# Relieving one DMA engine of 48 scattered rows, and marking the engines with fifteen small loads

## The chip, the cores and the metric

The kernel runs on one core of one Trainium2 chip. The metric is the device time of an execution in microseconds (us). Times are medians of several executions; a profile is one execution and gives the span from its first to its last instruction, some 2 us less than the timed value. Every timed run used below is in the fast state; a single look, which has too few runs to be placed, is marked so.

The engines are PE (matmul), DVE (vector), ACT, POOL (GpSimd) and SP (sync). The profile counts sixteen DMA engines. The trace records every DMA packet with its queue, its size and its duration, but not the number of its engine. A row that is copied from HBM to HBM (10,240 bytes) shows up as 16 packets of 640 bytes and 16 of 4 bytes (768 rows on q10 are 12,288 of each in the kernel before), which I read as one of each on every engine, the small one for its semaphore. A row that is scattered is one packet of 10,240 bytes (116 scatters of 128 rows are 14,848), and so on one engine.

## The reference

```python
x = np.random.randn(8, 2048, 2560).astype(np.float32)
scores = np.random.randn(8, 2048).astype(np.float32)
order = np.argsort(scores, axis=1)
ranks = np.argsort(order, axis=1)
out[b_idx, ranks, :] = x          # each row goes to the place of its rank
```

Every row of x (10,240 bytes) is read once and written once, to a place that is known only when the rank is known. That is 168 MB read and 168 MB written, so the kernel lives on its DMA engines.

## The kernel before

Each batch of 2048 rows is cut into eight groups of 256. Group 0 of batches 0 to 5 goes HBM to HBM, row by row, issued by SP and ACT (768 rows each, queues q1 and q10). The other 58 groups ("tiles") go through SBUF: POOL loads 128 partitions of 2 rows each, then scatters them in two indirect DMAs of 128 rows (queue q0). The ranks are counted by DVE.

```python
    GROUPS = [(256 * i, 2) for i in range(8)]
    DIRECT = range(6)
    BULK = [(b, g) for b in range(B) for g in range(len(GROUPS)) if g or b not in DIRECT]
    NBUF = 8
    LAG = 4
    G = 16
    ...
        for b in DIRECT:
            for h, (line, name) in enumerate(((sp, ENG.SP), (act, ENG.Activation))):
                line.after(dve, t_rows[b])
                half = WIDE // 2
                with line.eng.Fori(0, half // G) as q:
                    _, at = nc.values_load_multi_w_load_instructions(rows_i[b][...], ...)
                    for i in range(G):
                        row = b * N + GROUPS[0][0] + half * h + i
                        line.eng.dma_start(
                            out=out_bytes[bass.ds(at[i], ROW)],
                            in_=x_bytes[bass.ds(q * (G * ROW) + row * ROW, ROW)],
                        ).then_inc(s_rows[line], 16)
        for line in (sp, act):
            line.wait(s_rows[line], 16 * len(DIRECT) * WIDE // 2)
    ...
        def scatter(k, j):
            ...
            nc.gpsimd.indirect_dma_start(
                out=out_flat,
                out_offset=bass.IndirectOffsetOnAxis(ap=rank_i[:, col:col + 1], axis=0),
                in_=xb[k % NBUF][:, j * D:(j + 1) * D],
                in_offset=None,
                element_offset=b * N * D,
            ).then_inc(s_scat[k % NBUF][j], 16)
    ...
        for k, (b, g) in enumerate(BULK):
            i = k % NBUF
            if k >= LAG and k + NBUF - LAG < len(BULK):
                scatters_done(pl, k - LAG)
                load(pl, k + NBUF - LAG, s_load[(k - LAG) % NBUF])
            ...
            for j in range(GROUPS[g][1]):
                scatter(k, j)
        nc.gpsimd.drain()

        for k in range(max(0, len(BULK) - NBUF), len(BULK)):
            scatters_done(sp, k)
```

Of the kernel before, what the change touches and what calls it, by code (L numbers as in the profile page):

```python
# [7 lines left out]
P = 128  # L8
F32 = mybir.dt.float32
BF16 = mybir.dt.bfloat16  # L10
I32 = mybir.dt.int32
U8 = mybir.dt.uint8
OP = mybir.AluOpType
ENG = mybir.EngineType
# [26 lines left out]
def kernel(  # L41
# [6 lines left out]
    nc = tc.nc  # L48
    B, N, D = x.shape
    C = N // P  # L50
    ROW = 4 * D
# [4 lines left out]
    GROUPS = [(256 * i, 2) for i in range(8)]  # L56
    DIRECT = range(6)
    MMAX = max(m for _, m in GROUPS)
    WIDE = GROUPS[0][1] * P
    BULK = [(b, g) for b in range(B) for g in range(len(GROUPS)) if g or b not in DIRECT]  # L60
    NBUF = 8
    LAG = 4
    G = 16

    STEPS = [(0, 1), (1, 2), (2, 4), (4, 8)]

    def first_col(g):
        return GROUPS[g][0] // P if g < len(GROUPS) else C
# [11 lines left out]
    acc = [pool.tile([P, B * C], F32, name=f"acc{i}") for i in range(3)]  # L80
    rank = pool.tile([P, B * C], F32, name="rank")
    rank_i = pool.tile([P, B * C], I32, name="rank_i")
    rows_i = {b: pool.tile([1, WIDE], I32, name=f"rows_i{b}") for b in DIRECT}
    xb = [pool.tile([P, MMAX * D], F32, name=f"x{i}") for i in range(NBUF)]
    ps_col = psum.tile([P, 512], F32, name="ps_col")
# [7 lines left out]
    with tc.tile_critical(no_gpsimd_drain=True):  # L93
# [9 lines left out]
            [nc.alloc_semaphore(f"scat{i}_{j}") for j in range(MMAX)]  # L103
            for i in range(NBUF)
        ]
        s_rows = {sp: nc.alloc_semaphore("rows_sp"), act: nc.alloc_semaphore("rows_act")}
        n_scat = [[0] * MMAX for _ in range(NBUF)]

# [66 lines left out]
        def broadcast(b):  # L175
            pe.after(dve, t_copied)
            ticks = []
            for c in range(C):
                pe.did(
                    nc.tensor.transpose(  # L180
                        out=ps_all[:, P * c:P * (c + 1)],
                        in_=s_col[:, c, b:b + 1].to_broadcast([P, P]),
                        identity=ident[:],
                    )
                )
                if c % 4 == 3:
                    ticks.append(pe.n)
            return ticks
# [3 lines left out]
        dve.after(pl, t_mask)  # L192
        bc = broadcast(0)

        def ranks(b, g_lo, g_hi):

            for g in range(g_lo, g_hi):
                lo = first_col(g)
                m = GROUPS[g][1]
                for j in range(m):  # L200
                    col = b * C + lo + j
                    score = s_col[:, lo + j, b:b + 1]
                    dve.after(dve, dve.n)

                    def count(i, lo_c, hi_c, do, **how):
                        dve.did(
                            do(  # L207
                                out=trash[i][:, :P * (hi_c - lo_c)],
                                in0=s_all[:, P * lo_c:P * hi_c],
                                accum_out=acc[i][:, col:col + 1],  # L210
                                **how,
                            )
                        )

                    count(
                        0, lo, C, nc.vector.tensor_scalar,
                        scalar1=score, scalar2=None, op0=OP.is_lt, op1=OP.add,
                    )
                    if lo:
                        count(  # L220
                            1, 0, lo, nc.vector.tensor_scalar,
                            scalar1=score, scalar2=None, op0=OP.is_le, op1=OP.add,
                        )
                    count(
                        2, lo, lo + m, nc.vector.scalar_tensor_tensor,
                        scalar=score,
                        in1=mask[:, MMAX - j:MMAX - j + m, :].rearrange("p a b -> p (a b)"),
                        op0=OP.is_equal, op1=OP.mult,
                    )
            cols = slice(b * C + first_col(g_lo), b * C + first_col(g_hi))  # L230
            dve.after(dve, dve.n)
            dve.did(
                nc.vector.tensor_tensor(  # L233
                    out=rank[:, cols], in0=acc[0][:, cols], in1=acc[1][:, cols], op=OP.add
                )
            )
            dve.after(dve, dve.n)
            dve.did(
                nc.vector.tensor_tensor(  # L239
                    out=rank[:, cols], in0=rank[:, cols], in1=acc[2][:, cols], op=OP.add  # L240
                )
            )
            dve.after(dve, dve.n)
            tick = dve.did(
                nc.vector.tensor_copy(out=rank_i[:, cols], in_=rank[:, cols])  # L245
            )
            for g in range(g_lo, g_hi):
                t_bulk[b, g] = tick

        def rows_to_psum(b):  # L250
            pe.after(dve, dve.n)
            for j in range(GROUPS[0][1]):
                pe.did(
                    nc.tensor.transpose(  # L254
                        out=ps_row[:1, P * j:P * (j + 1)],
                        in_=rank[:, b * C + j:b * C + j + 1],
                        identity=ident[:],
                    )
                )

        def rows_to_bytes(b):
            dve.after(pe, pe.n)
# [11 lines left out]
        for b in range(B):  # L274
            dve.after(dve, dve.n)
            for q in range(4):
                dve.after(pe, bc[q])
                t_copied = dve.did(
                    nc.vector.tensor_copy(  # L279
                        out=s_all[:, 512 * q:512 * (q + 1)],  # L280
                        in_=ps_all[:, 512 * q:512 * (q + 1)],
                    )
                )
            steps = STEPS if b == 0 else [(0, len(GROUPS))]
            for lo, hi in steps:
                ranks(b, lo, hi)
                if lo == 0:
                    if b in DIRECT:
                        rows_to_psum(b)
                        rows_to_bytes(b)  # L290
                    if b + 1 < B:
                        bc = broadcast(b + 1)


        for b in DIRECT:
# [4 lines that stand above are left out]
                    _, at = nc.values_load_multi_w_load_instructions(  # L300
                        rows_i[b][:, bass.ds(half * h + q * G, G)],
                        engines=[name],
                        min_val=b * N * ROW,
                        max_val=(b * N + N - 1) * ROW,
                        skip_runtime_bounds_check_because=(
                            "a rank counts other scores of one batch of N, so it lies in 0..N-1"
# [5 lines that stand above are left out]
                            out=out_bytes[bass.ds(at[i], ROW)],  # L312
                            in_=x_bytes[bass.ds(q * (G * ROW) + row * ROW, ROW)],
                        ).then_inc(s_rows[line], 16)
        for line in (sp, act):
            line.wait(s_rows[line], 16 * len(DIRECT) * WIDE // 2)


        def scatters_done(line, k):
# [4 lines left out]
        def scatter(k, j):  # L324
            b, g = BULK[k]
            col = b * C + first_col(g) + j
            n_scat[k % NBUF][j] += 1
# [3 lines that stand above are left out]
                in_=xb[k % NBUF][:, j * D:(j + 1) * D],  # L331
                in_offset=None,
                element_offset=b * N * D,
            ).then_inc(s_scat[k % NBUF][j], 16)

        for k in range(1, NBUF):
            load(pl, k, s_load[k])
        for k, (b, g) in enumerate(BULK):
            i = k % NBUF
            if k >= LAG and k + NBUF - LAG < len(BULK):  # L340
                scatters_done(pl, k - LAG)
                load(pl, k + NBUF - LAG, s_load[(k - LAG) % NBUF])
            if k == 0:
                pl.wait(s_first, 16)
            else:
                pl.wait(s_load[i], 16 * (k // NBUF + (i > 0)))
            pl.after(dve, t_bulk[b, g])
            for j in range(GROUPS[g][1]):
                scatter(k, j)
        nc.gpsimd.drain()  # L350

        for k in range(max(0, len(BULK) - NBUF), len(BULK)):
            scatters_done(sp, k)

# [29 lines left out]
```

## Time and profile before

| | before |
|---|---|
| median of 2 runs | 793.37 us (792.85 to 793.88) |
| profiled span | 791.4 us |
| last scatter packet ends | 786.68 us |
| landings of a scatter near 757 us, against the middle one: first, 15th, 16th | -0.9, +3.4, +23.1 us |
| packets of 10,240 bytes (scatters) | 14,848, mean 386.8 ns |
| one row: 640-byte packet, its 4-byte packet | 32 ns, 9 ns |

The third row and those below it are read from the packet records and the semaphore landings, not from the page. A scatter's semaphore has 16 landings, read here as one by each of the 16 engines, so they show how far apart the engines are. (A scatter is named here by the time of its middle landing; how far the last one is behind that is called its lag.) Here fourteen are together, one is 3 to 4 us behind, one is 23 us behind. The page's slices and the stretches that belong to this are shown inside the prediction. Two further lines are needed later. The first is from the waits of SP (line, releaser: total us, times, longest): at the end SP waits 2.9 us in the closing barrier for POOL.

```profile
SPq L93 <- POOLq L93: 2.9, 1, 2.9
```

The second is a stretch in the middle. Its columns are the stretch, its length, the busy time of PE, PEld, DVE, ACT and POOL, the granted clock, the DMA share, and GB/s.

```profile
395.00:406.00 11.00, 0.00 (x0) 0.00 (x0) 10.86 (x25) 0.00 (x0) 2.70 (x3) 0.50 1.01 419
```

The DMA engines are full there: share 1.01, 419 GB/s. (The share is the packets' time over that of 16 engines; a packet starts some 3 ns before the one ahead of it ends, so full engines read a little over 1.) That is the ordinary rate of this kernel.

### The profile page before, as it was taken

How to read it: one execution, taken by the hardware profiler on the slowest of the kernel's cores; microseconds unless marked ns; L12 is line 12 of the kernel's file. 1: busy time of each engine (PE TensorE's matmuls, PEld its weight loads, DVE VectorE, ACT ScalarE, POOL GpSimd, SP SyncE). 2: the span in 40 equal slices, each digit the busy share in tenths (PEclk: the TensorE clock that was granted, in tenths of full speed). 3: DMA queues.
4: the chain of work that ended last, by engine and by line, in shares of the span. 5: the costliest groups of instructions: out<-in, count | busy, mean ns of one | idle time of the engine just before them, and what ended most of it. 6: DMA issues, size and time to landing. Idle time of an engine off the chain costs nothing.

```text
span 791.4 us, 7991 instructions
## 1 busy us (share of the span) xinstructions
PE 30.9 (4%) x156; PEld 27.6 (3%) x156; DVE 398.3 (50%) x809; ACT 0.0 (0%) x1; POOL 146.2 (18%) x182
## 2 busy tenths in 40 slices
PE   4000010020100200200000000000000000000000
PEld 3000010010100100200000000000000000000000
DVE  5999999999999999999992000000000000000000
ACT  0000000000000000000000000000000000000000
POOL 2114021212121211112121212121111212121000
PEclk9655555555555555655555555555555555555555
DMA  8999999999999999999999999999999999999960
GB/s 366 423 407 416 425 416 423 418 425 415 427 414 425 415 424 416 425 420 422 419 419 421 420 422 420 422 418 423 418 424 419 422 419 423 418 425 418 417 252 19
DMA packets 74239, 320.12 MB, mean 404 GB/s; under 512 B 27368, under 2 KB 51944, under 8 KB 51944
## 3 DMA queue, kind: packets, MB, share of 16 engines
q0 software_dynamic: 24912, 301.48, 89.5%
q1 hardware_dynamic: 24736, 10.60, 4.9%
q10 hardware_dynamic: 24576, 7.91, 4.0%
q14 instruction: 14, 0.11, 0.0%
q8 instruction: 1, 0.02, 0.0%
HBM read 167.84 MB, written 167.77 MB: 424 GB/s over the span
## 4 chain that ended last, share of the span: by engine, by line
DVE 43%; another core or an unknown queue 30%; POOL 8%; DMA 6%; issue 6%; PE 3%; POOLq 0%; SPq 0%
DVE trash L207 41%; POOL out_dram L328 6%; DMA x<-in_x_dram 6%; PE ps_all L180 2%; POOL x L112 2%; DVE s_all L279 1%; PE ps_row L254 0%; DMA s_in<-in_scores_dram 0%; PE ps_col L159 0%; DVE rank_i L245 0%; DVE rank L239 0%; DVE rank L233 0%; POOLq L350 0%; POOLq L28 0%
## 5 line engine op out<-in xcount | busy, mean ns | idle before, releaser
L207 DVE TENSOR_SCALAR_CACHE_REDUCE trash<-s_all,s_col 128x1792 bf16<-128x1792 f32 (+7 forms) x240 | 315.2, 1348 | 4.6
L328 POOL DMA_INDIRECT out_dram<-x,rank_i x116 | 112.3, 968 | 146.1 <-DVE rank_i L245 55.7
L112 POOL DMA_DIRECT2D x<-in_x_dram x57 | 32.1, 566 | 462.2 <-DMA out_dram<-x,rank_i 441.1
L207 DVE SCALAR_TENSOR_TENSOR trash<-s_all,s_col,mask 128x256 bf16<-128x256 f32 x128 | 61.6, 481 | 0.0
L180 PE MATMUL ps_all<-ident,s_col 128*128 128x128 f32 x128 | 26.5, 394 | 1.2 <-DVE s_all L279 0.8
L180 PEld LDWEIGHTS ps_all<-ident,s_col 128*128 128x128 f32 x128 | 25.1, 214 | 2.0 <-DVE s_all L279 1.1
L279 DVE COPY s_all<-ps_all 128x512 f32<-128x512 f32 x32 | 21.4, 689 | 6.0 <-PE ps_all L180 5.3
L207 DVE DVE_READ_ACCUMULATOR trash<-s_all,s_col 128x1 f32 x240 | 19.9, 83 | 0.0
L254 PE MATMUL ps_row<-ident,rank 128*1 128x128 f32 x12 | 3.5, 396 | 288.9 <-DVE rank_i L245 288.9
L207 DVE DVE_READ_ACCUMULATOR trash<-s_all,s_col,mask 128x1 f32 x128 | 10.7, 83 | 0.0
L254 PEld LDWEIGHTS ps_row<-ident,rank 128*1 128x1 f32 x12 | 0.5, 81 | 291.1 <-DVE rank_i L245 291.1
L264 DVE TENSOR_SCALAR rows_i<-ps_row 1x256 int32<-1x256 f32 x6 | 2.5, 411 | 4.1 <-PE ps_row L254 4.1
L167 DVE COPY s_col<-ps_col 128x128 f32<-128x128 f32 x1 | 0.3, 292 | 5.0 <-PE ps_col L159 5.0
L159 PE MATMUL ps_col<-ident,s_in 8*128 8x8 f32 x16 | 2.1, 264 | 4.1 <-DMA s_in<-in_scores_dram 4.1
L245 DVE CAST rank_i<-rank 128x16 int32<-128x16 f32 (+3 forms) x11 | 2.0, 180 | 0.4
L159 PEld LDWEIGHTS ps_col<-ident,s_in 8*128 8x128 f32 x16 | 2.0, 211 | 4.1 <-DMA s_in<-in_scores_dram 4.1
L239 DVE TENSOR_TENSOR rank<-rank,acc 128x16 f32<-128x16 f32 (+3 forms) x11 | 1.9, 170 | 0.4
L233 DVE TENSOR_TENSOR rank<-acc,acc 128x16 f32<-128x16 f32 (+3 forms) x11 | 1.9, 170 | 0.4
L140 POOL TENSOR_SCALAR_AFFINE_SELECT mask<-mask 128x256 f32<-128x256 f32 x2 | 0.8, 399 | 0.0
L152 DVE MEMSET acc<- 128x128 f32 x1 | 0.2, 165 | 1.1 <-SPq L93 1.1
L123 POOL MEMSET mask<- 128x512 f32 x1 | 0.5, 525 | 0.0
L122 POOL MEMSET ident<- 128x128 f32 x1 | 0.2, 204 | 0.5 <-SPq L93 0.5
(6 smaller groups left out, 0.7 us busy)
## 6 DMA issues: line engine op xcount, KB each, us to landing
x<-in_x_dram POOLq DMA_DIRECT2D x57, 2560.0 KB, 46.3
out_dram<-in_x_dram ACTq DMA_DIRECT2D x768, 10.0 KB
out_dram<-in_x_dram SPq DMA_DIRECT2D x768, 10.0 KB
x<-in_x_dram SPq DMA_DIRECT2D x1, 2560.0 KB, 13.2
out_dram<-x,rank_i POOLq DMA_INDIRECT x116, 51.2
s_in<-in_scores_dram SPq DMA_DIRECT2D x1, 64.0 KB
```

The lines of the kernel that those rows point to most:

```text
L112: line.eng.dma_start(out=xb[k % NBUF][:, :m * D], in_=x[b, r:r + P * m, :].rearrange("(p j) d -> p (j d)", j=m),).then_inc(sem, 16)
L140: nc.gpsimd.affine_select(out=part, in_=part, pattern=[[0, MMAX], [-1, P]], compare_op=OP.is_ge, fill=0.0, base=-half, channel_multiplier=1,)
L159: nc.tensor.transpose(out=ps_col[:, B * c:B * (c + 1)], in_=s_in[:, r + j:r + m * P:m], identity=ident[:B, :B],)
L180: nc.tensor.transpose(out=ps_all[:, P * c:P * (c + 1)], in_=s_col[:, c, b:b + 1].to_broadcast([P, P]), identity=ident[:],)
L207: do(out=trash[i][:, :P * (hi_c - lo_c)], in0=s_all[:, P * lo_c:P * hi_c], accum_out=acc[i][:, col:col + 1], **how,)
L233: nc.vector.tensor_tensor(out=rank[:, cols], in0=acc[0][:, cols], in1=acc[1][:, cols], op=OP.add)
L239: nc.vector.tensor_tensor(out=rank[:, cols], in0=rank[:, cols], in1=acc[2][:, cols], op=OP.add)
L245: nc.vector.tensor_copy(out=rank_i[:, cols], in_=rank[:, cols])
L254: nc.tensor.transpose(out=ps_row[:1, P * j:P * (j + 1)], in_=rank[:, b * C + j:b * C + j + 1], identity=ident[:],)
L264: nc.vector.tensor_scalar(out=rows_i[b][:].rearrange("o (p j) -> o p j", p=P), in0=ps_row[:1, :WIDE].rearrange("o (j p) -> o p j", p=P), s ...
L279: nc.vector.tensor_copy(out=s_all[:, 512 * q:512 * (q + 1)], in_=ps_all[:, 512 * q:512 * (q + 1)],)
L328: nc.gpsimd.indirect_dma_start(out=out_flat, out_offset=bass.IndirectOffsetOnAxis(ap=rank_i[:, col:col + 1], axis=0), in_=xb[k % NBUF][:, ...
```

## The change

The intent: one engine ends some 24 us after the rest, so in three tiles of batch 6 the rows of the eight partitions that are taken to be its own (64 to 67 and 96 to 99) are not scattered. Their index is raised by N and the scatter has a bounds check that skips it. Leaving these rows out is called thinning below. The 48 rows go HBM to HBM instead, issued by SP (32) and ACT (16) after all their other rows. Fifteen small loads of different sizes ("marks") are put into POOL's stream, so that a trace could tell which packets belong to which engine. The prediction calls the engine that was assumed for these partitions engine 8; that is a name, the trace has no numbers of engines.

```diff
+    MARKS = [(2, 32 + 3 * i) for i in range(8)]
+    MARKS += [(3, 65)] + [(2, 68 + 3 * i) for i in range(5)] + [(3, 86)]
+    THIN = [(6, 5), (6, 6), (6, 7)]
+    FIRST = 64
+    HOLES = [FIRST + 32 * h + i for h in range(2) for i in range(4)]
 ... (hole = N at those partitions, made from ident by DVE; added to the indices of the three tiles)
 ... (thin_i: the true byte offsets of the 48 rows, by a transpose on PE and one operation on DVE)
+        for n, (b, g) in enumerate(THIN):
+            line, name = ((sp, ENG.SP), (act, ENG.Activation))[n % 2]
+            line.after(dve, t_rows[b, g])
+            _, at = nc.values_load_multi_w_load_instructions(thin_i[b, g][:], ...)
+            for i in range(len(HOLES) * m):
+                row = b * N + r + HOLES[i % len(HOLES)] * m + i // len(HOLES)
+                line.eng.dma_start(out=out_bytes[bass.ds(at[i], ROW)],
+                    in_=x_bytes[bass.ds(row * ROW, ROW)]).then_inc(s_rows[line], 16)
 ... (in scatter)
+                **(dict(bounds_check=N - 1, oob_is_err=False) if (b, g) in THIN else {}),
 ... (in the loop over tiles)
+            if k == 28:
+                at = 0
+                for w, n in MARKS:
+                    nc.gpsimd.dma_start(out=scratch[:w, at:at + n], in_=x[0, :w, :n]).then_inc(s_mark, 16)
+                    at += n
 ... (at the end)
+        sp.wait(s_mark, 16 * len(MARKS))
```

More of the change, by code (lines that the diff above doesn't have):

```diff
@@ L82 @@
     rank_i = pool.tile([P, B * C], I32, name="rank_i")
+    hole = pool.tile([P, 1], F32, name="hole")
+    thin_i = {k: pool.tile([1, len(HOLES) * MMAX], I32, name=f"thin_i{k[0]}_{k[1]}") for k in THIN}
+    scratch = pool.tile([3, 1024], F32, name="scratch")
     rows_i = {b: pool.tile([1, WIDE], I32, name=f"rows_i{b}") for b in DIRECT}
@@ L105 @@
         ]
+        s_mark = nc.alloc_semaphore("mark")
         s_rows = {sp: nc.alloc_semaphore("rows_sp"), act: nc.alloc_semaphore("rows_act")}
@@ L193 @@
         bc = broadcast(0)
+        dve.did(
+            nc.vector.tensor_reduce(
+                out=hole[:],
+                in_=ident[:].rearrange("p (a h i) -> p a h i", a=2, h=2)[
+                    :, FIRST // 64, :, FIRST % 32:FIRST % 32 + 4
+                ],
+                axis=mybir.AxisListType.XY,
+                op=OP.add,
+            )
+        )
+        dve.after(dve, dve.n)
+        dve.did(
+            nc.vector.tensor_scalar(
+                out=hole[:], in0=hole[:], scalar1=float(N), scalar2=None, op0=OP.mult
+            )
+        )
         def ranks(b, g_lo, g_hi):
@@ L248, in ranks, with rows_to_psum @@
                 t_bulk[b, g] = tick
-        def rows_to_psum(b):
+                if (b, g) in THIN:
+                    cols = slice(b * C + first_col(g), b * C + first_col(g + 1))
+                    dve.after(dve, dve.n)
+                    t_bulk[b, g] = dve.did(
+                        nc.vector.tensor_scalar(
+                            out=rank_i[:, cols],
+                            in0=rank[:, cols],
+                            scalar1=hole[:],
+                            scalar2=None,
+                            op0=OP.add,
+                        )
+                    )
+        def rows_to_psum(b, g):
             pe.after(dve, dve.n)
-            for j in range(GROUPS[0][1]):
+            for j in range(GROUPS[g][1]):
+                col = b * C + first_col(g) + j
                 pe.did(
@@ L255, in rows_to_psum @@
                         out=ps_row[:1, P * j:P * (j + 1)],
-                        in_=rank[:, b * C + j:b * C + j + 1],
+                        in_=rank[:, col:col + 1],
                         identity=ident[:],
@@ L259, in rows_to_psum, with thin_to_bytes @@
                 )
+        def thin_to_bytes(b, g):
+            m = GROUPS[g][1]
+            dve.after(pe, pe.n)
+            t_rows[b, g] = dve.did(
+                nc.vector.tensor_scalar(
+                    out=thin_i[b, g][:].rearrange("o (j h i) -> o j h i", j=m, h=2),
+                    in0=ps_row[:1, :P * m].rearrange("o (j a h i) -> o j a h i", j=m, a=2, h=2)[
+                        :, :, FIRST // 64, :, FIRST % 32:FIRST % 32 + 4
+                    ],
+                    scalar1=float(b * N),
+                    scalar2=float(ROW),
+                    op0=OP.add,
+                    op1=OP.mult,
+                )
+            )
         def rows_to_bytes(b):
@@ L288 @@
                     if b in DIRECT:
-                        rows_to_psum(b)
+                        rows_to_psum(b, 0)
                         rows_to_bytes(b)
@@ L292 @@
                         bc = broadcast(b + 1)
+                for g in range(lo, hi):
+                    if (b, g) in THIN:
+                        rows_to_psum(b, g)
+                        thin_to_bytes(b, g)
         for b in DIRECT:
@@ L314 @@
                         ).then_inc(s_rows[line], 16)
+        n_rows = {line: len(DIRECT) * WIDE // 2 for line in (sp, act)}
+        for n, (b, g) in enumerate(THIN):
+            line, name = ((sp, ENG.SP), (act, ENG.Activation))[n % 2]
+            r, m = GROUPS[g]
+            line.after(dve, t_rows[b, g])
+            _, at = nc.values_load_multi_w_load_instructions(
+                thin_i[b, g][:],
+                engines=[name],
+                min_val=b * N * ROW,
+                max_val=(b * N + N - 1) * ROW,
+                skip_runtime_bounds_check_because=(
+                    "a rank counts other scores of one batch of N, so it lies in 0..N-1"
+                ),
+            )
+            for i in range(len(HOLES) * m):
+                row = b * N + r + HOLES[i % len(HOLES)] * m + i // len(HOLES)
+                line.eng.dma_start(
+                    out=out_bytes[bass.ds(at[i], ROW)],
+                    in_=x_bytes[bass.ds(row * ROW, ROW)],
+                ).then_inc(s_rows[line], 16)
+                n_rows[line] += 1
         for line in (sp, act):
-            line.wait(s_rows[line], 16 * len(DIRECT) * WIDE // 2)
+            line.wait(s_rows[line], 16 * n_rows[line])
         def scatters_done(line, k):
```

## The prediction

> **What bounds the kernel now.** I read the page first: the slices, the queues, then the waits, and at last the stretches of the end. The DMA engines are full from the second slice to the 38th, DVE has ended by the middle, and POOL spends most of its time waiting for scatters to land so that it can load the next tile.
>
> ```profile
> DVE  5999999999999999999992000000000000000000
> ...
> DMA  8999999999999999999999999999999999999960
> GB/s 366 423 407 416 425 416 423 418 425 415 427 414 425 415 424 416 425 420 422 419 419 421 420 422 420 422 418 423 418 424 419 422 419 423 418 425 418 417 252 19
> ...
> q0 software_dynamic: 24912, 301.48, 89.5%
> q1 hardware_dynamic: 24736, 10.60, 4.9%
> q10 hardware_dynamic: 24576, 7.91, 4.0%
> ...
> POOL x L112 <- DMA out_dram<-x,rank_i: 441.1, 45, 11.5
> ```
>
> The last two slices (20 us each) are the only loose ones: 252 and 19 GB/s. Their stretches, and what SP does there:
>
> ```profile
> 600.00:700.00 100.00, 0.00 (x0) 0.00 (x0) 0.00 (x0) 0.00 (x0) 19.33 (x23) 0.50 1.02 421
> 760.00:766.00 6.00, 0.00 (x0) 0.00 (x0) 0.00 (x0) 0.00 (x0) 0.00 (x0) 0.50 0.65 262
> 766.00:787.00 21.00, 0.00 (x0) 0.00 (x0) 0.00 (x0) 0.00 (x0) 0.00 (x0) 0.50 0.07 27
> ...
> SPq L28 <- DMA out_dram<-x,rank_i: 26.3, 8, 3.7
> ...
> 743.06 17.26 SPq L311 DMA_DIRECT2D out_dram<-in_x_dram  x17
> ...
> L311 SPq DMA_DIRECT2D out_dram<-in_x_dram x768: 447/521/2196, 19.9 to 759.6; - x192
> ...
> L300 SPq TENSOR_LOAD <-rows_i x48: 972/1664/3726, 18.5 to 744.0; - x48
> ```
>
> From 766 to 787 us the DMA share is 0.07, about one engine of sixteen. The packet records of the trace say the same: fourteen engines post their last packet between 762.8 and 764.4 us, one at 767.1, the last one at 786.75. The landings of each scatter show how that lag grew: the sixteenth engine lands 1 to 2 us after the first until 70 us, then 6.4 us at 205, 13.8 at 415, 20.8 at 625 and 24.1 at 750. The cause can be seen in the packet times: a 10,240-byte scatter packet takes 385 ns, but some 730 of 14,848 take 393 to 450, and wherever I could follow the engines from packet to packet (to 200 us, next start 3 to 4 ns before the previous end) practically all of these were on one engine. 928 scatter packets on it times some 28 ns is 26 us, which is the lag. So one engine, and only with its scatters, sets the end.
>
> The second thing to see is SP. Its row copies are issued until 760.3 us, one per 0.98 us at the end, although an unblocked one takes 0.74 us. Some issues take up to 2.2 us instead of 0.52[...]. At 760 us the slow engine still has some 34 rows of SP's queue before it[...].
>
> [...] The trace before has no engine numbers. [...] while the slow engine is alone, each 385 ns scatter packet is followed by one packet of q1 (32 ns or 9 ns) and one of q10, and all three queues run dry together at 786.73 to 786.75 us.
>
> **The change part by part.** Removed: 3 groups x 2 scatters x 8 partitions = 48 scatter packets of one engine. On the slow one each is worth about 413 - 4 ns, so 48 x 0.41 = 19.7 us: just the lag. The loads of those partitions stay. If engine 8 is the slow one, and if a skipped row is really dropped without the rest being dealt out anew over the engines, its scatters would end at 786.7 - 19.7 = 767.0 us, beside the others.
>
> Added on every engine: 48 rows of one 640-byte packet and one 4-byte one, 28 + 6 ns net = 1.6 us in all. The fifteen marks put one or two small packets and fifteen 4-byte ones on each engine, some 0.2 us. On POOL the marks cost 15 x (0.56 + 0.3) = 13 us once, near 395 us; a load lands 46 us after its issue, and the fast engines, 13 us ahead of the slow one then, still have more than 20 us queued. This is hidden. DVE gains two small operations at the start and six in batch 6 (0.2 to 0.4 us each), PE six transposes; both are over by 460 us, the rows are needed after 600. Hidden.
>
> What isn't hidden is where the 48 rows are issued. SP and ACT [...] issue them after all 768 rows of their own. SP gets two of the three groups, 32 rows, and two register loads. Each row costs 0.57 us (the 521 ns issue and its gap) to 0.74 us (as in the loop, with its address arithmetic): 18 to 24 us. Each register load takes 1.0 to 1.7 us: 2 to 3.4 us.
>
> When does SP begin? Its last old row goes out when the slow engine has taken all but 34. This engine takes one q1 packet per q0 packet. The 48 dropped q0 packets save 19.7 us, but the same number of q1 packets must then go beside 48 later q0 packets of 0.41 us or more, so SP gets there hardly earlier: 756 to 760 us. Until the engine's scatters run dry at 767 SP is still held to about 0.83 us a row for some ten rows, which costs another 2 to 3 us. So the last row is issued at about 757 + 2.5 + 21 + 2.5 = 783 us (779 to 787). On idle engines the load of the scores took 3.0 us from issue to landing: 786 us. SP then needs some 0.6 us for its remaining waits, and from its last wait to the end before took 791.4 - 787.1 = 4.3 us; the timed runs lie 2.0 us over the span (793.4 against 791.4). Sum: 786 + 0.6 + 4.3 + 2.0 = 792.9 us. The 20 us that leave the slow engine come back as 20 us of serial issue on SP.
>
> **The rivals.** First, the full gain: the end is 767 + 1.6 + 7 = 775.5 us, 2.3% faster. For it speaks that bytes are that well balanced; against it that SP cannot have issued 32 rows by then unless it reached them by about 745 us[...]. Second, engine 8 is not the slow engine, or skipping deals the rows out over all engines: the slow engine keeps its scatters, gets 1.6 us of row packets more, and still throttles SP at 0.83 us a row until its queue is within 34 rows of the end. The last issue is then about 787, the landing 789 to 791, the time 795.5 to 797.5. [...] against it that the number of thinned rows matches the lag so well that the writer seems to know the engine. I give the slow engine's being thinned 0.55. Third, a skipped row costs POOL or the engines as much as a written one: same time as the second. Fourth, the marks starve the engines: up to 13 us more, 806 us; the queued 20 us speak against it.
>
> **Range and chances.** 0.55 x 792.7 + 0.45 x 796 = 794.2; I say 794. The two main cases lie within 4 us, and the unknown row issue (0.57 to 0.74 us, 32 rows) is worth 5 us: 789.5 to 798.5. Faster by over 2% needs 777.5 us, hence the first rival: 0.04. Slower by over 2% needs 809 us: 0.02. Within 2%: 0.94.
>
> **What would show it.** Right, if the page of the kernel after has the last issue of the new rows on SP at 779 to 788 us and SP's last wait there is for rows, not scatters. If engine 8 was the slow one, the sixteenth landing of the last scatter comes within 6 us of the first instead of 24, before 770 us, and 14,800 packets of 10,240 bytes remain (48 fewer); in the other case the lag of about 24 us stands. It is wrong if SP issues the 32 rows in much less than 18 us or finishes its old rows before 750 us (then the gain shows), or if the GB/s row has a dent near 395 us (then the marks cost).

## The result, and the profile after

The kernel after takes 803.1 us (median of 2 runs, 802.5 to 803.69) and is correct. The ratio to the kernel before is 1.0123, with a 95% interval of 1.0079 to 1.0166. Ratios here are the mean time of one kernel's fast runs over that of the other's of the same rounds, so not quite the ratio of the medians quoted. It is within 2%, the likeliest class, but 9.7 us slower and outside the predicted range of 789.5 to 798.5.

The page after, the rows that answer to those in the prediction:

```profile
DVE  5999999999999999998991000000000000000000
...
DMA  8999999999999999999999999999999999999950
GB/s 367 426 408 415 424 419 417 422 417 424 417 424 418 425 415 426 415 426 413 336 360 413 427 415 425 415 423 419 422 420 420 422 418 415 420 420 421 401 218 20
...
q0 software_dynamic: 25392, 300.99, 89.0%
q1 hardware_dynamic: 25760, 10.93, 5.4%
q10 hardware_dynamic: 25088, 8.08, 4.5%
```

The dent is in slices 20 and 21: 336 and 360 GB/s instead of 419 and 419. This is the sign that the prediction had named for "the marks cost". Queue q0 has 480 packets more although 48 rows fewer are scattered. 480 is 15 x 2 x 16, which reads as two packets of each mark on each of the 16 engines. Counted by size, 32 of them carry the rows that the marks load and 448 have 4 bytes, which reads as an engine without data getting a small packet all the same, beside the one for the semaphore. That accounts for all 480, so the 48 skipped rows are not gone. There are 14,800 packets of 10,240 bytes (48 fewer), and of 4 bytes 3,264, which is 2,768 before, 448 of the marks and 48 more. **A skipped row becomes a packet of 4 bytes.**

The stretches around the dent and at the end:

```profile
340.00:395.00 55.00, 1.76 (x6) 0.26 (x6) 52.11 (x110) 0.00 (x0) 17.88 (x27) 0.50 1.02 420
395.00:406.00 11.00, 0.00 (x0) 0.00 (x0) 10.86 (x23) 0.00 (x0) 2.49 (x3) 0.50 1.43 165
406.00:440.00 34.00, 0.00 (x0) 0.00 (x0) 16.97 (x39) 0.00 (x0) 4.98 (x6) 0.50 1.02 413
...
776.00:787.00 11.00, 0.00 (x0) 0.00 (x0) 0.00 (x0) 0.00 (x0) 0.00 (x0) 0.50 0.12 34
787.00:798.00 11.00, 0.00 (x0) 0.00 (x0) 0.00 (x0) 0.00 (x0) 0.00 (x0) 0.50 0.06 22
```

From 395 to 406 us only 165 GB/s move, although the share of busy time rises to 1.43. The engines are not short of work, they are full of packets that take long and carry little. What is missing against the kernel before is (419 - 165) / 419 of 11 us, or 6.7 us. From 787 to 798 us the picture is that of the kernel before from 766 to 787: one engine alone, share 0.06.

POOL's own line for the marks, from its timeline (start, length, line, operation):

```profile
358.84 7.75 POOL L426 DMA_DIRECT2D scratch<-in_x_dram  x15
```

The issue took 7.75 us, less than the 13 predicted, and it began 36 us before the dent. POOL is not what makes the dent. In the packet records the marks are reached by the engines from 395 to 406 us, and there the small packets are long: from 396 to 401 us a 4-byte packet of q0 takes 134 ns on average and a 640-byte row packet 100 ns (q1) or 114 ns (q10), against 9 and 32 ns in the kernel before.

The end, seen from SP: its waits, then the timeline and the group of the new rows (group columns: duration in ns min/median/max, first and last start).

```profile
SPq L28 <- DMA out_dram<-x,rank_i: 15.1, 5, 3.7
SPq L102 <- DMA out_dram<-in_x_dram: 3.4, 1, 3.4
...
SPq L102 <- POOLq L102: 0.4, 1, 0.4
```

```profile
749.51 4.42 SPq L371 DMA_DIRECT2D out_dram<-in_x_dram  x4
...
756.27 25.04 SPq L391 DMA_DIRECT2D out_dram<-in_x_dram  x32
...
L391 SPq DMA_DIRECT2D out_dram<-in_x_dram x32: 517/539/1465, 756.3 to 780.8; - x32
```

SP issues the new rows from 756.3 to 780.8 us, which is where the prediction had put them, and the last DMA that it waits for is one of rows. But the issue isn't what sets the end: the last row is issued at 780.8 and the scatters go on until 796.09 us.

The landings of single scatters, from the semaphore records (us against the middle landing):

```
                              first   second   15th    16th
before, scatter at 757.3 us    -0.9    -0.9    +3.4   +23.1
after,  scatter at 758.9 us   -13.5    -1.5    +3.7   +24.6
```

Relieving some engine worked, but not the right one. One engine is now 13.5 us ahead of the others, and the slow one is as far behind as before.

### The profile page after: what moved, and what is told of

The parts are those of the page before. It is cut to its first block, busy times and chain, and to the rows that moved or that the text cites. A ratio compares the mean times of both kernels' runs of the same rounds, so it can differ in the third digit from the quotient of the medians.

```text
span 802.0 us, 8134 instructions
## 1 busy us (share of the span) xinstructions
PE 32.5 (4%) x162; PEld 27.7 (3%) x162; DVE 399.9 (50%) x817; ACT 0.0 (0%) x1; POOL 153.9 (19%) x197
## 4 chain that ended last, share of the span: by engine, by line
another core or an unknown queue 48%; POOL 14%; DVE 12%; DMA 12%; issue 8%; PE 1%; POOLq 0%; SPq 0%
DVE trash L234 12%; POOL out_dram L409 10%; DMA out_dram<-x,rank_i 6%; DMA x<-in_x_dram 6%; POOL x L122 3%; POOL scratch L426 1%; PE ps_all L190 0%; DVE s_all L335 0%; DMA s_in<-in_scores_dram 0%; PE ps_col L169 0%; POOLq L438 0%; DVE rank_i L272 0%; DVE rank L266 0%; DVE rank L260 0%
## 5 line engine op out<-in xcount | busy, mean ns | idle before, releaser
L122 POOL DMA_DIRECT2D x<-in_x_dram x57 | 32.2, 567 | 464.9 <-DMA out_dram<-x,rank_i 464.9
L294 PE MATMUL ps_row<-ident,rank 128*1 128x128 f32 x18 | 5.3, 396 | 335.9 <-DVE rank_i L272 289.1
L234 DVE DVE_READ_ACCUMULATOR trash<-s_all,s_col,mask 128x1 f32 x128 | 10.6, 83 | 0.0
L426 POOL DMA_DIRECT2D scratch<-in_x_dram x15 | 7.7, 525 | 0.0
```

The costliest lines, as they stand in the source:

```text
L122: line.eng.dma_start(out=xb[k % NBUF][:, :m * D], in_=x[b, r:r + P * m, :].rearrange("(p j) d -> p (j d)", j=m),).then_inc(sem, 16)
L234: do(out=trash[i][:, :P * (hi_c - lo_c)], in0=s_all[:, P * lo_c:P * hi_c], accum_out=acc[i][:, col:col + 1], **how,)
L294: nc.tensor.transpose(out=ps_row[:1, P * j:P * (j + 1)], in_=rank[:, col:col + 1], identity=ident[:],)
L426: nc.gpsimd.dma_start(out=scratch[:w, at:at + n], in_=x[0, :w, :n]).then_inc(s_mark, 16)
```

## The experiments

Two theories stood after the result. **Theory A**: the marks cost about 7 us by uncovered small packets, and the 48 rows cost the rest, some 2 to 3 us, because they pile up on a slow engine that was not relieved. **Theory B**, the rival: the thinning or POOL's longer stream delays everything (POOL waits longer for scatters, 464.9 us instead of 441.1), and marks and rows are secondary. Nine kernels ran (e1 to e9; they are told by question, not by number); all that are timed had the kernel before beside them in the same rounds.

### Marks and rows apart: e1, e2, e3

e1 is the kernel after without the marks.

```diff
-    MARKS = ...            (with s_mark, scratch, the fifteen loads and SP's wait)
```

> The changed kernel without the fifteen marks. Theory (the marks cost 7 to 8 us when the engines reach them near 396 us, the 48 rows cost 2 us because the engine that was thinned is not the slow one): 795 to 796.5 us, ratio to before 1.003, no dent in GB/s near 400 us, last scatter landing still about 24 us after the others. Rival (the marks are harmless, the rows at the end of SP's queue cost the 10 us): 801 to 804 us.

Measured 801.34 us (4 runs, 800.77 to 801.55), ratio 1.0099 [1.0082, 1.0116], correct. The expectation was a clear miss: without the marks, 8 of the 9.7 us are still there. The time lies in the range of its rival, but the rival's first half, that the marks are harmless, falls with e2.

e2 is the kernel before with the burst of marks and nothing else.

```diff
+            if k == 28:
+                at = 0
+                for w, n in MARKS:
+                    nc.gpsimd.dma_start(out=scratch[:w, at:at + n], in_=x[0, :w, :n]).then_inc(s_mark, 16)
```

> The kernel before with only the fifteen marks added, in one burst. Theory: 800.5 to 801.5 us (7 to 8 us over before), with two slices of 330 to 360 GB/s near 400 us. Rival (marks harmless): 793 to 794 us.

Measured 800.08 us (799.9 to 800.82), ratio 1.0089 [1.0072, 1.0106]; a little under the expected range. Its stretch shows the dent without any thinning:

```profile
395.00:406.00 11.00, 0.00 (x0) 0.00 (x0) 10.86 (x25) 0.00 (x0) 2.49 (x3) 0.50 1.47 171
```

So the marks alone cost 6.7 us, or 0.45 us for each. With two packets of each mark on every engine, that is some 0.22 us a packet. No run parts the marks' few data packets from their 4-byte ones.

e3 spreads the same marks, one ahead of each of tiles 28 to 42.

```diff
+            if 28 <= k < 28 + len(MARKS):
+                w, n = MARKS[k - 28]
+                at = sum(c for _, c in MARKS[:k - 28])
+                nc.gpsimd.dma_start(out=scratch[:w, at:at + n], in_=x[0, :w, :n]).then_inc(s_mark, 16)
```

> The same fifteen marks, but one ahead of each of fifteen successive tiles instead of a burst. If what costs is that many tiny transfers stand one behind the other in every engine's queue, with nothing large between them to cover their latency, this costs 0 to 1.5 us (793.5 to 795). If each mark has a fixed cost of its own (0.5 us each), it stays at 800 to 801 us. If it was POOL's 8 us of issuing in one go, it is 793.5 too, but then the dent of e2 would begin at the issue and not 30 us later.

Measured 796.44 us (795.76 to 796.72), ratio 1.0037 [1.002, 1.0054]. It missed the expected range: each mark still costs 0.2 us, 3.1 us together and twice the most that I had allowed, where I had thought that spread marks would nearly vanish between the large packets. In the packet records of e3 the 4-byte and 640-byte packets have their usual means of 9.0 and 32.1 ns, so the cost isn't in the small packets. It is in the loads behind them: of the 20,480-byte load packets between 370 and 620 us, 141 take over 900 ns, where the kernel before has 2 in that stretch and a median of 761. Summed up, these loads take 46.6 us longer than there, and on 16 engines that is 2.9 us for each on average, practically the whole 3.1. Packing the marks costs more than twice as much as spreading them.

### What a row costs, and where: e9, e1 against e7

e7 is e1 without the 48 copies (wrong on purpose: 48 rows are missing). Sent with e5 and e6, below.

```diff
-                line.eng.dma_start(...)   (the 48 row copies)
```

> Wrong on purpose: the changed kernel without marks and without the 48 row copies, still thinned at 64. Theory: the dropped rows of an engine that isn't the last are worth nothing, 793 to 794.5 us, so that the whole 8 us of e1_no_marks over the kernel before are the 48 row copies. Rival (dropping itself costs POOL or the engines): 796 to 801.

Measured 793.88 us (793.58 to 794.08) against 793.87 for the kernel before, ratio 1.0002 [0.9986, 1.0019]. The sixteenth landing lags by 23.8 us. Dropping 48 rows of partitions 64 to 67 and 96 to 99 changes nothing, neither for better nor for worse. This rules out one half of theory B: the thinning, its DVE and PE work and the bounds check cost nothing. (Its other half, POOL's longer stream, fell with the dent, which e2 has without any thinning, 36 us after POOL's issue.) And the 48 copies cost 801.34 - 793.88 = 7.5 us, or, by the kernels before of the two sets (793.35 and 793.87), 8.0 us.

Where they cost it can be seen in e1: SP's waits, then the end in three stretches.

```profile
SPq L98 <- DMA out_dram<-in_x_dram: 9.1, 1, 9.1
SPq L28 <- DMA out_dram<-x,rank_i: 3.3, 1, 3.3
```

```profile
740.00:764.00 24.00, 0.00 (x0) 0.00 (x0) 0.00 (x0) 0.00 (x0) 3.60 (x4) 0.50 0.98 394
764.00:789.00 25.00, 0.00 (x0) 0.00 (x0) 0.00 (x0) 0.00 (x0) 0.00 (x0) 0.50 0.18 47
789.00:799.00 10.00, 0.00 (x0) 0.00 (x0) 0.00 (x0) 0.00 (x0) 0.00 (x0) 0.50 0.04 2
```

In the last stretch 2 GB/s move. The slow engine serves its queues one packet each in turn: in the records of the kernel before, from 767.4 us, each of the 46 scatter packets (385 ns) is followed by one packet of q1 and one of q10. There its q0 and its rows run dry together, at 786.73 to 786.75 us. With 48 rows more, 48 row packets are left when the last scatter packet has ended at 788.40 us. From then on the records of e1 read like this (start, ns, queue, bytes):

```
790.760  342  q1   640
791.096   36  q10  640
791.128    9  q1     4
791.134    9  q10    4
791.140  342  q1   640
```

The first seven pairs of rows after the last scatter packet still take 68 ns each. From the eighth on a pair takes 380 ns, and once q10 is empty, a row takes 190 ns on average. The 48 packets need until 795.47 us, 7.1 us, and SP's last row lands 2.9 us later. SP's issue isn't what holds them up: it is over at 785.5 us, before the last scatter packet ends, and the records that follow have no gap between packets.

e9 tests whether the number of rows is what counts, without changing the thinning: as many rows are left out of batch 5 (32 on SP, 16 on ACT) as are added, so the total of row packets is that of the kernel before (wrong on purpose).

```diff
+                left = (2, 1)[h] if b == 5 else 0
-                with line.eng.Fori(0, half // G) as q:
+                with line.eng.Fori(0, half // G - left) as q:
```

> Wrong on purpose: as e1_no_marks (thinned at 64, 48 row copies at the end of the two queues, no marks), but of batch 5 the last 32 rows on SP and the last 16 on ACT are not copied, so that each queue issues as many rows as before. Theory (what costs 8 us in e1 is the 48 rows more than the scatters can cover, not the rows as such nor their place at the end): 793 to 795 us, and after the last scatter's landing nothing is left over. Rival (the new rows come late because SP and ACT issue them after all others): 798 to 802 as in e1.

Measured 794.44 us (793.85 to 795.45), kernel before 793.24, ratio 1.0011 [0.9995, 1.0028]. No row packet comes after the last scatter packet. The register loads and the 48 rows at the end of the two queues are all still there, and cost some 1 us or nothing. But e9 doesn't keep their lateness: with as many rows less ahead of them, SP issues its 32 rows some 30 us earlier than in e1. SP's timeline in e1, then in e9:

```profile
763.39 22.14 SPq L386 DMA_DIRECT2D out_dram<-in_x_dram  x32
```

```profile
732.50 30.50 SPq L387 DMA_DIRECT2D out_dram<-in_x_dram  x32
```

So e9 alone would leave the late issue as a rival. e1's own records settle it, as said above: all rows were issued before the scatters ended. What costs is the number of rows, once it exceeds what the slow engine has scatters to hide.

### Which engine: e4, then e5 and e6

e4 drops, in each of tiles 28 to 43, the rows of another eight partitions, assumed to be those of one engine: 0 to 3 and 32 to 35 in tile 28, then four further on from tile to tile, up to 28 to 31 and 60 to 63 in tile 35; 64 to 67 and 96 to 99 in tile 36, and so on up to 92 to 95 and 124 to 127 in tile 43. There are no copies (wrong on purpose).

```diff
+    THIN = {(BULK[28 + i]): e for i, e in enumerate([0, 1, ..., 15])}
+    hole = pool.tile([P, 16], F32, name="hole")     # column e: N at the partitions that tile 28 + e drops
```

> Wrong on purpose: in sixteen successive tiles (28 to 43) the scatters drop the eight partitions of one engine [...], and nothing copies the dropped rows. The lag of the sixteenth landing behind the others should fall by 6 to 7 us at one tile alone, that of the slow engine, and stay at about 0.4 us of growth per tile elsewhere; the end comes some 6 us earlier. [...] Rival (dropping deals rows out over all engines): no single fall.

One run, 790.5 us, state unknown, so the time isn't used. The landings of scatters and of the loads between them give the answer:

```
middle landing              15th landing   16th landing     (us against the middle)
442.1 us, a load               +5.0          +15.0
445.4 us, tile 31              +3.6          +15.4
448.9 us, tile 31              +1.9          +15.4
455.1 us, a load               +1.7          +15.6
458.6 us, tile 32              +1.5          +14.0
461.8 us, tile 32              +1.7          +12.8
468.4 us, a load               +1.5          +12.1
```

The lag of the second-slowest engine falls at one tile alone, tile 31 (from 5.0 to 1.9 us): partitions 12 to 15 and 44 to 47. That of the slow one falls at the next, tile 32 (from 15.6 to 12.1 us): **partitions 16 to 19 and 48 to 51.** At tile 36, which drops the partitions of the change, nothing happens to it. 16 dropped rows bring 3.5 us, or 0.2 us a row, half of what I expected. Every other tile puts one more engine about 3 us ahead. The 256 dropped rows are 256 more packets of 4 bytes. The trace shows the partitions of the slow engine, not its number. The records are those of e4 only, but e5 and e6 test the reading with another tile set.

e5 is e1 with the right partitions, e6 is e5 without the copies (wrong on purpose).

```diff
-    FIRST = 64
+    FIRST = 16
```

> The changed kernel without marks, thinned at partitions 16-19 and 48-51 (those whose drop lowered the slow engine's lag) instead of 64-67 and 96-99. Theory (a dropped row still costs a 4-byte packet and its round of 0.2 us, so it saves 0.2 us and not 0.41; a row left over after the last scatter costs 0.2 us): the slow engine's last scatter lands 10 us earlier than without marks at 64, near 779 us, then some 9 us of left-over rows: 790 to 793 us in all. Rival (the right engine brings the 20 us): 774 to 778. Rival (nothing but SP's serial issue sets the end): 801 as at 64.

> Wrong on purpose: as e5_port16, but the dropped rows are copied by nobody. Theory: 48 x 0.2 = 10 us under the kernel before, 782 to 785 us, and the last scatter's sixteenth landing 13 to 14 us behind the others instead of 24. If a dropped row saved its whole 0.41 us: 773 to 775.

e6 took 783.65 us (783.6 to 783.73), ratio 0.9873 [0.9857, 0.989]; the lag is 13.3 us. Against e7, which differs in FIRST alone, the same 48 rows are worth 793.88 - 783.65 = 10.2 us on these partitions and nothing on the others. That confirms the engine. It also confirms the price: 10.2 / 48 = 0.21 us a row, about half of the 0.41 that a scatter packet takes with its two companions.

e5 took 791.66 us (791.49 to 792.01), ratio 0.9975 [0.9959, 0.9992]. Correct, but of the 10.2 us the copies take 8.0 back, by the same mechanism as in e1: 48 row packets come after the last scatter packet, which ends at 778.42 us. Here too SP had issued its last row before, at 773.4 us, and the expectation's second rival, that SP's serial issue alone sets the end (801 us), is ruled out. Even on the right engine the change without its marks gains 0.25%.

### A version that beats both: e8

The lesson of e5 and e9 is that the number of rows must not rise. e8 keeps it: half of the direct group of batch 5 (128 rows) goes back into a tile, and its 128 places are given to rows of the slow engine (seven tiles, 16 rows each) and of the second-slowest (the eighth tile). Against the kernel before (skip, true offsets and row copies are as in the kernel after, without marks):

```diff
-    GROUPS = [(256 * i, 2) for i in range(8)]
-    DIRECT = range(6)
+    GROUPS = [(0, 1), (128, 1)] + [(256 * i, 2) for i in range(1, 8)]
+    DIRECT = {0: 2, 1: 2, 2: 2, 3: 2, 4: 2, 5: 1}
+    THIN = {(5, 3): 16, (5, 4): 16, (5, 5): 16, (5, 6): 16, (6, 3): 16, (6, 4): 16, (6, 5): 16, (6, 6): 12}
```

> A try at a better version: batch 5 sends only 128 rows straight from HBM to HBM instead of 256 (half a tile more for everyone, some 6.5 us), and the 128 row copies so freed take the rows of the slow engine in seven tiles and of the second-slowest (partitions 12-15 and 44-47) in one. The number of row copies is that of the kernel before, so none is left over at the end. Theory: slow engine 786.7 + 6.6 - 7 x 3.3 = 770, all others 770, so 775 to 779 us. If the left-over rows weren't the reason of e1's 8 us, it is 784 or more.

Measured **778.16 us** (777.88 to 778.63), ratio 0.9806 [0.979, 0.9823] to the kernel before: 15.7 us faster, correct. (At the threshold of 2% the verdict is unclear, since the interval spans it; that it is faster is clear.) The page and the end:

```profile
DMA  8999999999999999999999999999999999999996
GB/s 366 422 406 415 424 417 424 416 421 420 425 414 423 418 421 422 422 420 416 425 416 425 419 415 421 422 426 406 410 423 424 420 410 413 419 423 422 419 415 280
```

```profile
740.00:770.00 30.00, 0.00 (x0) 0.00 (x0) 0.00 (x0) 0.00 (x0) 1.67 (x2) 0.50 1.00 411
770.00:776.00 6.00, 0.00 (x0) 0.00 (x0) 0.00 (x0) 0.00 (x0) 0.00 (x0) 0.50 0.03 12
```

The engines are full into the last slice, instead of one running alone from 764 to 787 us. A scatter near 767 us lands within -0.9 to +1.7 us of the middle on all 16 engines.

## Why the prediction was wrong

| profiled, us | before | e1 | e2 | e9 | after | e8 |
|---|---|---|---|---|---|---|
| last scatter packet ends | 786.68 | 788.40 | 792.74 | 788.02 | 796.09 | 771.21 |
| row packets after it | 1 | 48 | 0 | 0 | 18 | 0 |
| span | 791.4 | 799.9 | 798.2 | 793.2 | 802.0 | 776.2 |

The span of the kernel after can be read off. Its scatters end 9.4 us later. Then 18 row packets take 1.3 us, to 797.38, and the last landing of SP's rows comes 2.9 us after them, where before the last scatter landed 0.4 us after its packet. In return the tail is shorter: 1.7 us from 800.3 to the end instead of 4.3, as POOL has drained while SP waited for its rows (0.4 us of barrier instead of 2.9). 9.4 + 1.3 + 2.5 - 2.6 = 10.6 us, the difference of the spans.

What held:

- The bound: one slow engine, by its scatters alone, sets the end. e6 (against e7) and e8 show it by taking rows from this engine.
- The work of DVE and PE and the rest of the thinning is hidden (e7: 793.88 against 793.87).
- The two signs that were to show the prediction right came true, and it was wrong all the same. The last issue of the new rows is at 780.8, in 779 to 788, but 783 had been worked out for a relieved slow engine and about 787 for the case that came about; that it fell inside is partly luck. And SP's last wait is for rows because their packets stood behind the slow engine's scatters, not because SP issued them late. A sign that a rival gives as well decides nothing.
- 48 scatter packets fewer, and the rivals named: the second, that another engine is the slow one and that its lag of 24 us stands, is what happened; the fourth, that the marks cost, came nearest in size.

What failed, step by step (the sum of 792.9 entered the prediction's mean as 792.7, which changes nothing). The first step alone takes the gain away but costs nothing against the kernel before (e7: 793.88 us). The second and third, both costs of small packets, made the 9.7 us.

1. **"If engine 8 is the slow one", at 0.55.** The slow one is not the engine of partitions 64 to 67 and 96 to 99 but that of 16 to 19 and 48 to 51 (in e4 the lag falls from 15.6 to 12.1 us there; e6 takes 783.65 us against 793.88 of e7). That the thinned engine is the slow one was my assumption; nothing in the trace before showed it. The closeness of 48 rows to the lag, which I took as a sign that the writer knew the engine, was no evidence.
2. **"The fifteen marks put ... some 0.2 us"** on each engine. They cost 6.7 us alone (e2). The term was worked out from 9 ns a packet, which is what the record of a small one reads between large ones in the kernel before. Thirty in a row on every engine (two for a mark) have nothing large between them; there (396 to 401 us) the 4-byte packets of q0, q1 and q10 take 115 to 168 ns on average. Spread out, the marks cost 3.1 us, which the loads behind them show (e3). The fourth rival had the size of this, but "the marks starve the engines" through POOL is not the cause: e2's dent is at 395 to 406 us with the engines busy, and POOL's issue lay 36 us earlier.
3. **"48 rows of one 640-byte packet and one 4-byte one, 28 + 6 ns net = 1.6 us in all".** They cost 7.5 to 8.0 us (e1 against e7, e5 against e6), since those beyond the slow engine's scatter packets run alone at its end: 48 packets, 7.1 us. e9, with the same thinning and the same rows at the end but no more rows in all, is back within about 1 us.
4. **"On the slow one each is worth about 413 - 4 ns", 19.7 us.** Even on the right engine it is 0.21 us (e6), so the third rival was half right. The records of e6 show where the rest goes. Of each run of 16 dropped rows the first 14 or so pass in some 40 ns a round; then the engine stalls, with 4-byte packets of up to 491 ns, for about 1 us, and the two loads that follow take 1.4 to 2.3 us instead of 0.76. Over the three runs the stalls make up 3.0 us and the loads 5.8, together 8.8 of the 9.5 us that are missing (19.7 - 10.2). The kernel before has no such packet in that stretch. So a row skipped takes its time later, in the same way as a spread mark.
5. **"The 20 us that leave the slow engine come back as 20 us of serial issue on SP."** Nothing left it, and SP's issue, over at 781.3 us, was hidden under scatters that went on until 796.09; so it was in e1 and e5. The prediction's 0.98 us a row at SP's end, which it read as SP being held back, includes a register load: one of the 16 gaps is 3.17 us, the other 15 have a mean of 0.89, and ten of them are the unblocked 0.74 to 0.76. That the slow engine holds SP's issue to 0.83 us a row (two of its rounds of 413 ns) was my estimate; no run shows it. The end was the slow engine's in every timed kernel but e8.

Marks and rows don't add up: 6.7 + 8.0 = 14.7 us apart, 9.7 together. The marks' thirty q0 packets gave the slow engine thirty more rounds, each with one packet of q1 and one of q10. A row is two packets there (640 and 4 bytes), so 15 rows of each queue found a place, 30 in all, and 48 - 30 = 18 were left at the end, as the records show. The count fits exactly; no run was made for it alone. These 18 take only 1.3 us because the first 13 pass at 34 ns each; only the last four take 180 to 193 ns.

Left open: why the slow engine's scatter packets are slow. 731 of the 14,848 packets take 393 to 450 ns, loads keep to their 761 (98 of 100 after 100 us), and the 46 scatter packets that start after 767.2 us, when the slow engine is alone, take 385 ns every one. In this trace, then, it was slow only beside the others; I have not separated the engine from its partitions. The last scatter packet of e1 and e9 came 1.7 and 1.3 us later than that of the kernel before, that of e7 only 0.2; this is from one profile each and I can't explain it. Nor did the marks name an engine: following the packets of the kernel after gives one chain with 128, 140, 152, 164 and 176 bytes at 84 to 86 ns spacing from 395.652 us, and a second with the same sizes from 396.492 us. This reads as the same two engines for each of these marks; if so, the marks could not tell the engines apart. The later ones were not followed.

## What to carry to other kernels

Cost a small DMA packet by what is queued beside it. Here its own record said 9 to 32 ns (kernel before), but in a burst it took 100 to 168 ns on average (kernel after, 396 to 401 us), at the drained end of a queue, after the first dozen or so, a 640-byte one took 180 to 193 ns (kernel after) or 342 (e1, with two queues left), and between large packets the time turned up in the loads behind it (e3, 46.6 us over 16 engines). Fifteen small loads that no one waits for took 6.7 us from all engines here (e2). When a queue is relieved in favour of another, keep the number of packets on the slow engine's other queues the same, as e8 did, or the surplus runs alone at the end (48 packets, 7.1 us, in e1). Ask of a sign that is to show a prediction right whether a rival would give it too. Before balancing an engine, find it by dropping the rows of another group of partitions in each tile and watching which landing moves; that took one kernel here, and with it the same idea gained 15.7 us instead of losing 9.7.
